# Second buffers for the operands of band attention, and half-size one-hot tiles for the expert gates, in a one-layer streaming encoder block

## The chip, the cores and the metric

One of the eight cores of a Trainium2 chip runs the whole program. The metric is the device time of one execution in microseconds (us); the result is told as the median of several runs. The five engines have queues of their own and run each queue strictly in order: PE (TensorE, matrix products), DVE (VectorE, elementwise work and reductions), ACT (ScalarE, activations and copies), POOL (GpSimd, which here only starts gathers) and SP (SyncE, which here starts every other transfer).

## The reference

The layer works on 1024 tokens of width 1024. Cut to what matters:

```python
h = modulate(rms_norm(x), shift1, scale1); proj = h @ w_in
o_a = chunked_band_attention(qa, ka, va)       # 8 heads of 64; a chunk of 64 sees itself and 8 before it
o_b = gated_delta_rule(conv(qkv_b), g, beta)   # 4 heads of 128, a state carried from chunk to chunk
x = x + gate1 * (concat(rms_norm(o_a), o_b) @ w_out)
h2 = modulate(rms_norm(x), shift2, scale2)
# experts: 8 heads pick 16 of 16384 single-neuron experts for each token
u, vv = expert_down[experts], expert_up[experts]
y = einsum("thk,thkd->td", gates * gelu(einsum("thkd,td->thk", u, h2)), vv)
out = x + gate2 * y
```

All matrices are float32.

## The kernel before

The 1024 tokens are eight tiles of 128. The program has two parts.

**The front** takes every tile through six stages, which the program calls lanes. P (`project`) makes the projections of one or two tiles and stores queries, keys and values to a scratch tensor `rec` in the chip's main memory. D (`delta`) is the gated delta rule of one tile, with the state from the tile before. M (`attention`) is the band attention of one tile. O (`output`) is the output projection, the second norm and the query projection. R (`choose`) picks the experts. Tiles 2 to 5 are dense: G (`gates_dense`) spreads their gates over all 16384 experts, into a scratch tensor `gd`. The other tiles gather the rows of their own experts, one row of 1024 numbers per token and slot: `down` (L901 gathers, L903 multiplies and sums) and then `up` (L915 gathers, L920 accumulates), 128 slots each. In the front stand `down` and `up` of tile 0 and `down` of tile 1.

**The dense part** runs all experts as matrix products for the four dense tiles (L982 and L1005) in 32 steps of four blocks of 128 experts, and beside them the gathers of tiles 1, 6 and 7. Its memory lies where the lanes' memory was.

The order of each queue is set when the program is built, by a scheduler: every lane has a priority (`PRI`, L56: M first, then D, O, P, R, G, and the gathers last), and the scheduler places the ready instruction of the best priority, as its own reckoning has it. On the chip nothing overtakes: an instruction that waits holds up all that stands behind it on its engine. A buffer of a lane is one slot of a named ring; its next tile may be written once the last reader of the tile before is done.

**Attention of one tile** (L510 to L569) runs four rounds, one for each pair of heads. A round loads queries, keys and values of its pair into `kv` (L517, L519; up to 11 blocks of 128 by 128) and the biases of the near band into `near` (L522), both rings of one slot. Then come the scores (L532), the bias and running maximum (L536), the exponential (L539), the transposes (L548, copied at L550), the product with the values (L556) and the scaled result (L559). The score products read `kv`, and L556 is its last reader. All of a tile's products go through one bank of PSUM (`BANKS`, M=1). L568 ends the tile. In the delta lane L663 ends the tile, and its ring `rg` had 12 slots (`RINGS`, 'D').

**The gates of a dense tile** (L851 to L885): for each block of 16 tokens, groups of `GQ` = 8 tokens are taken. Two one-hot tiles of 128 by 8x128 half-precision numbers are compared on DVE (L870); ACT scales one of them twice per token, by the upper and the lower part of the gate (L877); PE multiplies (L878, two products per token), and after every four tokens ACT copies the bank to `stg` (L881). After 16 tokens two transfers store `stg` (L885). A group takes four tiles of a ring of six (`RINGS`, 'G').

Of the kernel before, what the change touches and what calls it, by code (L numbers as in the profile page):

```python
# [20 lines left out]
F = mybir.dt.float32  # L21
BF = mybir.dt.float16
R = mybir.dt.float32r
# [7 lines left out]
P = 128  # L31
D = 1024
# [16 lines left out]
NROW = 3  # L49
NMORE = 4  # L50
NHELD = 2
RINGS = {'P': 4, 'D': 12, 'M': 4, 'O': 3, 'R': 2, 'G': 6}
XBUFS = {'P': 1, 'O': 2}
WBUFS = {'P': 4, 'O': 3}
STEP = 10000
# [7 lines left out]
SHIFT = {}  # L63
SLOPE = {}
BANKS = dict(P=2, D=2, M=1, O=2, R=1)
GQ = 8
GROUPS = [[0], [1, 2], [3, 4], [5, 6], [7]]
STARTS = [0, 16, 24] + [32 + 4 * k for k in range(5)] + [52 + k for k in range(8)]
LEVELS = (1, 2, 4, 8, 16, 32, 64)
# [49 lines left out]
def hybrid_layer(ctx, tc, a, out):  # L119
    nc = tc.nc  # L120
    V, A_, PE, G, SP = nc.vector, nc.scalar, nc.tensor, nc.gpsimd, nc.sync
# [34 lines left out]
    def lt(shape, dt, name, bufs, tag=None):  # L156
        return pools_[cur[0][0]].tile(list(shape), dt, name=name, tag=(tag or name) + cur[0], bufs=bufs)

    def rg(shape=(P, 512), dt=F):
        return lt(shape, dt, "rg", RINGS[cur[0]])  # L160

# [348 lines left out]
    def attention(t, mixT):  # L510
        m0 = max(0, 4 - t)
        nk = 5 - m0
        oa = rg()
        for p in range(4):
            cs = slice(p * P, (p + 1) * P)
            kv = lt([P, 11, P], F, "kv", 1)
            SP.dma_start(kv[:, 0, :], rec[QA, t][:, cs])  # L517
            for n, kind in ((1, KA), (6, VA)):
                SP.dma_start(kv[:, n + m0:n + 5, :],  # L519
                             rec[kind, t - 4 + m0:t + 1, :, cs].rearrange("m p c -> p m c"))  # L520
            near = lt([P, 2, 256], F, "near", 1)
            SP.dma_start(near, neard[:, 2 * p:2 * p + 2])  # L522
            ss_, rs = [], sm(2)
            for hh in range(2):
                hp = slice(hh * 64, hh * 64 + 64)
                s = lt([P, 640], F, "sx", 2)
                init = BIG
                for lo, hi, bias in ((m0, 3, farm[:, min(m0, 2) * P:]), (max(m0, 3), 5, near[:, hh, (max(m0, 3) - 3) * P:])):
                    if lo >= hi:
                        continue  # L530
                    ps = mm()
                    PE.matmul(ps[:, :(hi - lo) * P], kv[hp, 0, :],  # L532
                              kv[hp, 1 + lo:1 + hi, :].rearrange("p m c -> p (m c)"), start=True, stop=True,
                              skip_group_check=True)
                    mf = sm(1)
                    V.tensor_tensor_reduce(s[:, lo * P:hi * P], ps[:, :(hi - lo) * P], bias, -1.0, init, OP.add,  # L536
                                           OP.min, accum_out=mf)
                    init = mf
                A_.activation(s[:, m0 * P:], s[:, m0 * P:], AF.Exp, bias=mf, scale=-1.0, accum_out=rs[:, hh:hh + 1])  # L539
                ss_.append(s)  # L540
            yield
            blocks = [(hh, m) for hh in range(2) for m in range(m0, 5)]
            PT = {}
            for b0 in range(0, len(blocks), 4):
                part = blocks[b0:b0 + 4]
                pt = mm()
                for n, (hh, m) in enumerate(part):
                    PE.transpose(pt[:, n * P:(n + 1) * P], ss_[hh][:, m * P:(m + 1) * P], ident)  # L548
                d = rg()
                A_.activation(d[:, :len(part) * P], pt[:, :len(part) * P], AF.Copy)  # L550
                for n, bm in enumerate(part):
                    PT[bm] = d[:, n * P:(n + 1) * P]
            po = mm()
            for hh in range(2):
                for m in range(m0, 5):
                    PE.matmul(po[:, hh * 64:hh * 64 + 64], PT[hh, m], kv[:, 6 + m, hh * 64:hh * 64 + 64],  # L556
                              start=(m == m0), stop=(m == 4), skip_group_check=True)
            V.reciprocal(rs, rs)
            V.tensor_tensor(v3(oa[:, cs], 2), v3(po[:, 0:P], 2), b3(rs, AD), OP.mult)  # L559
            yield  # L560
        junk = rg()
        ss = sm(1)
        A_.activation(junk, oa, AF.Square, accum_out=ss)
        r = rsqrt(ss, 1, 1.0 / 512)
        A_.activation(oa, oa, AF.Copy, scale=r)
        ps = transpose4(oa)
        for j in range(4):
            A_.activation(mixT[:, j, :], ps[:, j * P:(j + 1) * P], AF.Copy, scale=mixg[:, j:j + 1])  # L568
        yield  # L569
# [281 lines left out]
    def gates_dense(t):  # L851
        e12, gt = GATE.pop(t)
        ps = mm()
        for n, src in enumerate((e12[:, 0], e12[:, 1], gt)):
            PE.transpose(ps[:, n * P:(n + 1) * P], src.rearrange("p h s -> p (h s)"), ident)

        keys = lt([P, 2, P], BF, "gkeys", 1)
        V.tensor_copy(keys, ps[:, 0:2 * P].rearrange("p (a b) -> p a b", a=2))
        parts = lt([P, 2, P], F, "gparts", 1)
        V.tensor_scalar(parts[:, 0, :], ps[:, 2 * P:3 * P], 16384.0, None, op0=OP.mult)  # L860
        ghalf = lt([P, P], BF, "ghalf", 1)
        V.tensor_copy(ghalf, parts[:, 0, :])
        V.tensor_tensor(parts[:, 1, :], parts[:, 0, :], ghalf, OP.subtract)
        for blk in range(8):
            stg = lt([P, P, 16], F, "stg", 1)
            for q in range(2):
                n0 = blk * 16 + q * GQ
                oh1, oh2, whi, wlo = (rg((P, GQ * P), BF).rearrange("p (n i) -> p n i", n=GQ) for _ in range(4))
                for oh, key in ((oh1, 0), (oh2, 1)):
                    V.tensor_tensor(oh, iota_n[:, None, :].to_broadcast([P, GQ, P]),  # L870
                                    keys[:, key, n0:n0 + GQ, None].to_broadcast([P, GQ, P]), OP.is_equal)
                for h in range(GQ // 4):
                    ps = mm()
                    for j in range(4):
                        n = 4 * h + j
                        for m, w in enumerate((whi, wlo)):
                            A_.activation(w[:, n, :], oh2[:, n, :], AF.Copy, scale=parts[:, m, n0 + n:n0 + n + 1])  # L877
                            PE.matmul(ps[:, j * P:(j + 1) * P], w[:, n, :], oh1[:, n, :], start=(m == 0),  # L878
                                      stop=(m == 1), skip_group_check=True)
                    c0 = GQ * q + 4 * h  # L880
                    A_.activation(stg[:, :, c0:c0 + 4], ps.rearrange("p (n i) -> p i n", i=P), AF.Copy,  # L881
                                  scale=2.0 ** -14)
                yield
            for hf in range(2):
                SP.dma_start(gd[DENSE.index(t) * 8 + blk, hf], stg[:, hf * 64:hf * 64 + 64, :])  # L885
# [209 lines left out]
```

## Time and profile before

| what | value |
|---|---|
| median of three runs | 3504.95 us |
| the three runs | 3506.4, 3490.28, 3504.95 us |
| the profiled execution | 3495.83 us, its span 3494.1 us |
| busy share of the span: PE, DVE, ACT, POOL | 86%, 78%, 38%, 37% |
| first product of the dense part | 1967.2 us after the span's start |
| TensorE clock granted, mean | 0.902 of full speed |

The span runs from the first to the last instruction. A busy time counts what an engine ran, not how well; a wait row names the engine and line that waited, and the one that came last of what it waited for. "Idle before" and waits of an engine matter only where that engine, or one that waits for it, sets the end. SPq is the queue of SP itself.

### The profile page before, as it was taken

The page shows a single profiled execution, that of the slowest core. Times are in us where ns is not written, and L with a number is a line of the kernel's source. Part 1 is how long each engine was busy: PE and PEld are TensorE (multiplying, and loading weights), DVE is VectorE, ACT ScalarE, POOL GpSimd, SP SyncE. Part 2 cuts the span into 40 slices and gives each one's busy share as a digit, 9 for nine tenths or more (in the row PEclk, how much of TensorE's full clock was granted, in tenths as well). Part 3 has the DMA queues.
Part 4 walks back from the last instruction along what each step waited for, and adds up shares of the span by engine and source line. Part 5 has one row for each costly group of instructions (what it writes and reads, how often), then busy time and mean ns, then how long its engine had stood idle before and what let it go on. Part 6 is the DMA issues. An engine that isn't in the chain of part 4 may idle for free.

```text
span 3494.1 us, 44943 instructions
## 1 busy us (share of the span) xinstructions
PE 3014.0 (86%) x15196; PEld 2482.1 (71%) x15196; DVE 2719.5 (78%) x6407; ACT 1316.2 (38%) x2833; POOL 1310.2 (37%) x1028
## 2 busy tenths in 40 slices
PE   7988868798887898576877699999999999999998
PEld 5677756677766787465756577877777777777777
DVE  3347668768899778993585888988888888889898
ACT  2333134233235663386767632222222222222222
POOL 0000333432333323430000155556655556655563
PEclk9988878899878899686878899999999999999999
DMA  8865888898777987773435699999999999999997
GB/s 283 284 215 174 274 282 267 270 336 280 261 250 230 354 297 261 258 250 125 157 119 176 218 345 334 344 341 339 328 330 336 344 337 349 335 333 355 344 332 283
DMA packets 375959, 989.71 MB, mean 283 GB/s; under 512 B 33440, under 2 KB 139296, under 8 KB 375728
## 3 DMA queue, kind: packets, MB, share of 16 engines
q0 software_dynamic: 147456, 536.94, 43.4%
q1 hardware_dynamic: 228272, 449.90, 37.6%
q8 instruction: 119, 1.95, 0.2%
q14 instruction: 112, 0.92, 0.1%
HBM read 924.84 MB, written 61.87 MB: 282 GB/s over the span
## 4 chain that ended last, share of the span: by engine, by line
PE 37%; DMA 26%; DVE 20%; issue 9%; ACT 5%; POOL 3%; SPq 0%; DVEq 0%; POOLq 0%; ACTq 0%
PE at L982 12%; DMA row<-in_peer_expert_down_dram,idx 8%; PE yk L1005 6%; PE mm L365 5%; PE yc L1005 4%; DVE row L903 4%; DMA row<-in_peer_expert_up_dram,idx 4%; DMA rawu<-in_peer_expert_up_dram 4%; DVE y L920 4%; PE mm L351 3%; DMA rawd<-_peer_expert_down_t_dram 2%; POOL row L901 2%; DMA g<-gd 2%; ACT rg L877 2%; DMA w<-in_w_ada_dram 1%
## 5 line engine op out<-in xcount | busy, mean ns | idle before, releaser
L901 POOL DMA_INDIRECT row<-in_peer_expert_down_dram,idx x512 | 645.5, 1261 | 1113.0 <-DVE s L310 353.7
L915 POOL DMA_INDIRECT row<-in_peer_expert_up_dram,idx x512 | 664.5, 1298 | 1035.5 <-DMA g<-gd 421.3
L903 DVE CUSTOM_DVE_ANT_0 row<-row,h2a 128x1024 f32<-128x1024 f32 x512 | 619.7, 1222 | 139.4 <-DMA row<-in_peer_expert_down_dram,idx 138.6
L920 DVE SCALAR_TENSOR_TENSOR y<-row,act,y 128x1024 f32<-128x1024 f32 x508 | 651.8, 1283 | 53.3 <-DMA row<-in_peer_expert_up_dram,idx 50.1
L877 ACT ACTIVATE rg<-rg,gparts 128x128 f16<-128x128 f16 x1024 | 318.3, 396 | 75.7 <-PE mm L878 49.0
L985 ACT ACTIVATE gl<-at 128x512 f32<-128x512 f32 x128 | 76.4, 597 | 670.8 <-PE at L982 670.8
L982 PE MATMUL at<-hhi,dhi 128*128 128x512 f32 x1024 | 260.6, 396 | 16.3 <-ACT dhi L963 16.2
L365 PE MATMUL mm<-h2T,w 128*128 128x256 f32 (+1 forms) x1280 | 251.8, 358 | 19.0 <-DMA w<-in_peer_w_query_dram 8.2
L982 PE MATMUL at<-hlo,dhi 128*128 128x512 f32 x1024 | 256.8, 392 | 0.0
L1005 PE MATMUL yk<-uhi,whi 128*128 128x512 f32 x512 | 202.5, 412 | 61.7 <-ACT whi L991 56.4
L351 PE MATMUL mm<-w,hT 128*128 128x256 f32 x1024 | 249.3, 398 | 7.3 <-DMA w<-in_w_in_dram 4.6
L982 PE MATMUL at<-hhi,dlo 128*128 128x512 f32 x1024 | 254.7, 389 | 0.7 <-DVE dlo L964 0.7
L365 PEld LDWEIGHTS mm<-h2T,w 128*128 128x128 f32 x1280 | 218.2, 205 | 44.7 <-DMA w<-in_peer_w_query_dram 9.7
L982 PEld LDWEIGHTS at<-hhi,dhi 128*128 128x128 f32 x1024 | 194.7, 191 | 60.1 <-ACT dhi L963 19.0
L351 PEld LDWEIGHTS mm<-w,hT 128*128 128x128 f32 x1024 | 199.2, 200 | 45.3 <-DMA w<-in_w_in_dram 6.4
L982 PEld LDWEIGHTS at<-hlo,dhi 128*128 128x128 f32 x1024 | 194.4, 190 | 41.0
L982 PEld LDWEIGHTS at<-hhi,dlo 128*128 128x128 f32 x1024 | 192.2, 188 | 41.0 <-DVE dlo L964 1.2
L1005 PE MATMUL yk<-ulo,whi 128*128 128x512 f32 x512 | 204.0, 404 | 3.5 <-DVE ulo L964 3.5
L1005 PE MATMUL yc<-uhi,whi 128*128 128x512 f32 x512 | 205.1, 401 | 0.5 <-DVE yacc L1014 0.5
L1005 PE MATMUL yc<-ulo,whi 128*128 128x512 f32 x512 | 204.2, 399 | 0.0
L1005 PE MATMUL yc<-uhi,wlo 128*128 128x512 f32 x512 | 199.5, 390 | 0.0
L870 DVE TENSOR_TENSOR rg<-iota_n,gkeys 128x1024 f16<-128x1024 f16 x128 | 151.0, 1222 | 55.9 <-PE mm L878 55.8
(300 smaller groups left out, 5582.1 us busy)
## 6 DMA issues: line engine op xcount, KB each, us to landing
w<-in_w_in_dram SPq DMA_DIRECT2D x140, 512.0 KB
rawd<-_peer_expert_down_t_dram SPq DMA_DIRECT2D x128, 512.0 KB
rawu<-in_peer_expert_up_dram SPq DMA_DIRECT2D x128, 512.0 KB
w<-in_peer_w_query_dram SPq DMA_DIRECT2D x80, 512.0 KB
gd<-stg SPq DMA_DIRECT2D x64, 512.0 KB
g<-gd SPq DMA_DIRECT2D x32, 1024.0 KB
w<-in_w_ada_dram SPq DMA_DIRECT2D x48, 512.0 KB
w<-in_w_out_dram SPq DMA_DIRECT2D x40, 512.0 KB
```

The source lines that it names most:

```text
L351: PE.matmul(ps[t][:, hf * 256:hf * 256 + 256], hT[:, k, tt * P:(tt + 1) * P], w[k], start=(k == 0), stop=(k == KD - 1), skip_group_check=True)
L365: PE.matmul(ps[:, (c % per) * W:(c % per + 1) * W], w[k][:, (c % 2) * P:(c % 2 + 1) * P], hT[:, k, :W], start=(k == 0), stop=(k == KD - 1) ...
L870: V.tensor_tensor(oh, iota_n[:, None, :].to_broadcast([P, GQ, P]), keys[:, key, n0:n0 + GQ, None].to_broadcast([P, GQ, P]), OP.is_equal)
L877: A_.activation(w[:, n, :], oh2[:, n, :], AF.Copy, scale=parts[:, m, n0 + n:n0 + n + 1])
L901: G.indirect_dma_start(out=r, out_offset=None, in_=a["peer_expert_down"], in_offset=bass.IndirectOffsetOnAxis(ap=idx[:, j:j + 1], axis=0))
L903: V.tensor_tensor_reduce(r, r, h2, 1.0, 0.0, OP.mult, OP.add, accum_out=act[:, j:j + 1])
L915: G.indirect_dma_start(out=row, out_offset=None, in_=a["peer_expert_up"], in_offset=bass.IndirectOffsetOnAxis(ap=idx[:, j:j + 1], axis=0))
L920: V.scalar_tensor_tensor(y, row, w[:, j:j + 1], y, op0=OP.mult, op1=OP.add)
L982: PE.matmul(ps, l[:, k, :], r[:, k, :], start=(n == 0), stop=(n == 3 * KD - 1))
L985: A_.activation(g, ps, AF.Gelu)
L1005: PE.matmul(ps, l[:, ts_], r[:, cs], start=(m == 0 and (s == 0 or not own)), stop=(m == 3 * SCN - 1 and (s == NK // SCN - 1 or not own)))
```

## The change

Three numbers and one loop bound change. `kv` and `near` get rings of two slots in place of one; this takes 7.5 KB of each partition's memory (5.5 and 2). The gate groups take `GQ` = 4 tokens in place of 8, so the six tiles of their ring have half the size (6 KB less), and a block of 16 tokens is four groups. The ring of the delta lane has 11 slots in place of 12 (2 KB less).

```diff
-RINGS = {'P': 4, 'D': 12, 'M': 4, 'O': 3, 'R': 2, 'G': 6}
+RINGS = {'P': 4, 'D': 11, 'M': 4, 'O': 3, 'R': 2, 'G': 6}
-GQ = 8
+GQ = 4
-            kv = lt([P, 11, P], F, "kv", 1)
+            kv = lt([P, 11, P], F, "kv", 2)
-            near = lt([P, 2, 256], F, "near", 1)
+            near = lt([P, 2, 256], F, "near", 2)
-            for q in range(2):
+            for q in range(16 // GQ):
                 n0 = blk * 16 + q * GQ
                 oh1, oh2, whi, wlo = (rg((P, GQ * P), BF).rearrange("p (n i) -> p n i", n=GQ) for _ in range(4))
```

The scheduler builds every queue anew, so instructions move on all engines. Two places show it.

On SP, the loads of the last attention round of the last tile (L517, L519), among the stores of gates (L885), the weights of the query projection (`w_query`) and of the output projection (`w_out`). Before:

```order
L198 DMA w<-in_w_out_dram 128x1024
L522 DMA near<-neard 128x512
L198 DMA w<-in_w_out_dram 128x1024 x2
L250 DMA rg<-gated 128x512
L885 DMA gd<-stg 128x1024 x2
L517 DMA kv<-rec 128x128
L519 DMA kv<-rec 128x5x128 x2
```

Now:

```order
L522 DMA near<-neard 128x512
L198 DMA w<-in_peer_w_query_dram 128x1024 x2
L885 DMA gd<-stg 128x1024 x2
L198 DMA w<-in_peer_w_query_dram 128x1024 x2
L517 DMA kv<-rec 128x128
L519 DMA kv<-rec 128x5x128 x2
L198 DMA w<-in_peer_w_query_dram 128x1024 x2
L885 DMA gd<-stg 128x1024 x2
L198 DMA w<-in_peer_w_query_dram 128x1024 x3
L198 DMA w<-in_w_out_dram 128x1024
```

The load has moved ahead of five loads of query weights and of the first output weights of tile 7, which stood in front of it.

On ACT, the seam between the last gates (L877, L881) and the first split weights of the dense part (`dhi`, L963), up to the first expert activation (L985). Before:

```order
L877 ACTIVATE rg<-rg,gparts 128x128 x6
L963 ACTIVATE dhi<-rawd 128x1024
L833 ACTIVATE gt<-gt 128x128
L881 ACTIVATE stg<-mm 128x128x4
L963 ACTIVATE dhi<-rawd 128x1024
L881 ACTIVATE stg<-mm 128x128x4
L963 ACTIVATE dhi<-rawd 128x1024
L985 ACT_TABLE_LOAD
```

Now:

```order
L963 ACTIVATE dhi<-rawd 128x1024
L877 ACTIVATE rg<-rg,gparts 128x128 x8
L833 ACTIVATE gt<-gt 128x128
L881 ACTIVATE stg<-mm 128x128x4
L877 ACTIVATE rg<-rg,gparts 128x128 x6
L881 ACTIVATE stg<-mm 128x128x4
L877 ACTIVATE rg<-rg,gparts 128x128 x2
L963 ACTIVATE dhi<-rawd 128x1024
L877 ACTIVATE rg<-rg,gparts 128x128 x4
L985 ACT_TABLE_LOAD
```

Before, no scaling (L877) and two copies (L881) stand behind the first `dhi`; now 56 scalings and eight copies do, most of them behind the rows shown here.

## Rows read from the trace of the kernel before

**Rows 1.** Stretches of the span: engine busy us (instructions), then granted clock, DMA share, GB/s.
```profile
0.00:340.00 340.00, 281.83 (x1844) 222.98 (x1844) 161.03 (x724) 104.72 (x238) 1.62 (x6) 0.93 0.71 239
340.00:1550.00 1210.00, 984.76 (x5326) 832.50 (x5327) 971.88 (x2915) 503.87 (x1215) 430.52 (x386) 0.85 0.81 276
1550.00:1967.00 417.00, 310.38 (x1877) 255.81 (x1875) 256.60 (x1040) 297.98 (x860) 8.85 (x3) 0.77 0.46 154
1967.00:3494.00 1527.00, 1437.04 (x6152) 1170.84 (x6152) 1330.03 (x1732) 409.63 (x522) 869.17 (x634) 0.98 0.93 334
```

**Rows 2.** Waits of DVE, 340 to 1550 us: total us, times, longest.
```profile
DVE row L903 <- DMA row<-in_peer_expert_down_dram,idx: 132.5, 93, 4.8
DVE y L920 <- DMA row<-in_peer_expert_up_dram,idx: 45.0, 37, 3.9
DVE sx L536 <- PE mm L532: 13.7, 13, 3.8
```

**Rows 3.** Chain that ended last, 1590 to 1615 us: start, us, what.
```profile
1593.25 4.54 PE mm L556 x20
1597.81 0.32 SPq L517
...
1598.19 3.32 DMA kv<-rec
...
1601.65 1.63 PE mm L532 x2
...
1608.96 0.48 ACT stg L881
...
1612.09 2.33 ACT rg L877 x8
```

**Rows 4.** PE in order of time, 1590 to 1830 us: start, us, then what it waited for.
```profile
1620.20 4.53 PE L556 MATMUL mm<-kv,rg 128*128 128x64 f32 x20 [1.01 <-ACT rg L550]
...
1646.57 0.91 PE L532 MATMUL mm<-kv 64*128 64x384 f32 x2
...
1789.35 4.53 PE L556 MATMUL mm<-kv,rg 128*128 128x64 f32 x20 [0.98 <-ACT rg L550]
...
1797.80 1.62 PE L532 MATMUL mm<-kv 64*128 64x384 f32 x2 [1.37 <-DMA kv<-rec]
```

**Rows 5.** Waits of SP's queue, whole span.
```profile
SPq L517 <- PE mm L556: 127.7, 26, 13.1
```

**Rows 6.** Groups by line and shape: count | busy us, mean ns | idle before.
```profile
L870 DVE TENSOR_TENSOR rg<-iota_n,gkeys 128x1024 f16<-128x1024 f16 x128 | 151.0, 1222 | 55.9 <-PE mm L878 55.8
...
L625 DVE TENSOR_TENSOR rg<-rg,level 128x512 f32<-128x512 f32 x48 | 32.9, 686 | 0.0
```

**Rows 7.** Stretches, L870 alone: us, DVE busy (instructions), clock, DMA.
```profile
340.00:1550.00 1210.00, 61.44 (x52) 0.85 0.81 276
1550.00:1967.00 417.00, 89.60 (x76) 0.77 0.46 154
```

**Rows 8.** PE in order of time, 1900 to 2010 us.
```profile
1967.20 3.55 PE L982 MATMUL at<-hhi,dhi 128*128 128x512 f32 x8 [1.69 <-ACT dhi L963]
...
1976.61 1.98 PE L982 MATMUL at<-hlo,dhi 128*128 128x512 f32 x8
```

**Rows 9.** Ends of delta (L663) and attention (L568): duration ns min/median/max, first and last start.
```profile
L663 ACT ACTIVATE mixT<-mm,mix_gain x8: 687/687/738, 180.2 to 1666.7; 128x512 f32<-128x512 f32 x8
...
L568 ACT ACTIVATE mixT<-mm,mix_gain x32: 347/361/386, 182.7 to 1837.6; 128x128 f32<-128x128 f32 x32
```

**Rows 10.** Waits of DVE, 1550 to 1967 us.
```profile
DVE rg L870 <- PE mm L878: 50.5, 20, 7.6
DVE rg L559 <- PE mm L556: 30.3, 3, 12.5
DVE sx L536 <- PE mm L532: 25.3, 12, 7.3
```

**Rows 11.** Waits of ACT, 1550 to 1967 us.
```profile
ACT rg L877 <- PE mm L878: 28.9, 17, 4.9
```

## The prediction, before the changed kernel was run

> **What bounds the kernel now.** I read the stretches first, because the span has four parts with different limits [rows 1]. Before 340 us the first tile is on its way and no gather runs yet. From 340 to 1550 us the 384 gathers of the front run. From 1550 to 1967 us the front ends without gathers. From 1967 us the dense part runs. [...]
>
> From 340 to 1550 us it is DVE. It is busy for 972 of 1210 us, which leaves 238 us idle, and 177.5 of those are waits for a gathered row, 132.5 for `down` and 45.0 for `up` [rows 2]. The reader should see what stands third: DVE waited only 13.7 us for the scores of attention. DVE runs in order, so attention can be late here by tens of us and DVE does other work meanwhile. [...] The dependences of the last tiles set the end: attention of tile 7 ends at 1837.6 us, its delta rule already at 1666.7 [rows 9], and output, choice and the last gates follow.
>
> **How attention is chained.** One round in the chain of waits [rows 3]: the product with the values runs from 1593.25 us for 4.54 us, SP starts the load at 1597.81, the third transfer lands 3.32 us after 1598.19, and the next scores start at 1601.65. From the end of one round's last product to the next round's first it is 3.9 us, and none of it is arithmetic. SP was itself held up by this: 26 times it stood at L517 until L556 was done, 127.7 us in all [rows 5], with every other load behind it.
>
> **The change part by part.** The sum is made against the profiled execution, 3495.8 us, which is 9.1 us below the median of the three runs.
>
> *Second slots, 1550 to 1967 us.* Five loads fall here, one for tile 6 and four for tile 7. From the end of L556 to the next L532 the gaps are 3.9 us at 1597.8, 21.8 us at 1624.7 (1620.20 plus 4.53 to 1646.57), and so on to 3.9 us at 1793.9; the first, the largest and the last are shown [rows 3, 4], and the five add to 43 us. In the 21.8 us PE had output work to do that was placed ahead, so not all of that gap is the load. The floor is five times 3.9, 19 us; the ceiling 43. I take 25, nearer the floor, since the other gaps are near it. SP's queue agrees in kind: the last load now stands ahead of six weight loads that stood in front of it. What is late next is the bank of PSUM, which L559 must empty before the next scores: it waited 30.3 us in this stretch, three times [rows 10], and that wait stays.
>
> *Second slots, 340 to 1550 us.* DVE sets the pace, so the gain is what DVE waited for attention: at most 13.7 us [rows 2]. The load is one part of what delayed those scores. Between 0 and 14 I take 10, since the load is the only part of a round that waits on no arithmetic. If the order of DVE's queue falls otherwise, the 177.5 us of gather waits can shift by some 20 us either way; that is in the range, not in the sum.
>
> *Second slots, before 340 us.* Tile 0 has three such loads, but this stretch is filled by weights (239 GB/s, PE busy 282 of 340 us [rows 1]). I take nothing, with up to 3 x 3.9 = 12 us as the other end; the weights hide it, and if they were there earlier the 12 us would come in.
>
> *Gate groups of four.* L870 goes from 128 instructions of 1024 elements, 1222 ns each, to 256 of 512. No row shows a half-precision compare of 512, so the bounds are half of 1222 (611) and the nearest row of that size, 686 ns for a float32 product of 512 [rows 6]. The pieces of 1024 cost the same as other elementwise work of that size, so I take 686: 2 x 686 - 1222 = 150 ns more for each old instruction. 52 of them lie in the DVE-bound stretch [rows 7]: 52 x 0.150 = 7.8 us on the path. 76 lie after it, 11.4 us, where DVE is 62% busy: 7 us. Together 15, between 0 and 19. ACT scales as often as before and copies as often, and PE multiplies as often; they cost nothing more.
>
> [...]
>
> *The seam.* 56 scalings and eight copies of the last gates now stand on ACT behind the first `dhi`, against two copies before. At 2.33 us for eight scalings and 0.48 us for a copy [rows 3] the extra is 16.3 + 6 x 0.48 = 19.2 us of ACT. The first four blocks give PE 12 x 1.98 = 24 us of L982 [rows 8] to do beside it, though PE needs ACT's `dhi` for each of them. The work is moved, not added. Cost between 0 and 19; I take 5. If PE runs out of L982, the load of the finished gates is what is late.
>
> *Delta ring of 11.* Delta of tile 7 ends 171 us before attention does [rows 9], and that cover pays for any wait for a slot. Nothing, and from the cover up to perhaps 10 us where its pieces hold up PE's queue.
>
> *Sum:* -25 - 10 + 15 + 5 = -15, so 3480.8 on the scale of the profiled execution, and 3489.9 on that of the median. I do not know on which of the two the new runs will lie, and predict the middle, **3485 us**, 0.57% below 3504.95. The measurement tells about 0.5%, 17.5 us, from no change.
>
> **The rivals.**
>
> *A. Attention's chain sets the whole front.* 26 of the 32 loads waited for the round before, and SP's 127.7 us of it [rows 5] are of the size of the loads. If it bounded the front, 28 loads after tile 0 at 3.9 us would come off: 109 us, 3387 on the profiled scale and 3391 in the middle between the scales. For it: delta, output and choice all wait on attention, and the end of tile 7's attention is what the end of the front hangs on. Against: DVE's waits for L536 are 13.7 us in 1210 [rows 2], so the 23 loads before 1590 us are covered. [...]
>
> *B. The hand-over of gate groups doubles; slower.* In the last stretch DVE stood 50.5 us, 20 times, at L870 until PE had freed a one-hot tile [rows 10], and ACT 28.9 us, 17 times, at L877 [rows 11]. If these waits come once per group, and not with the amount of work, twice the groups add up to 79 us. The ring still holds one and a half groups, but now in half the time. With DVE's 50.5 added and the rest of the sum as above it is 3480.8 + 50.5 = 3531, in the middle scale 3536; with both, 3565. It decides from the point where more than a third of these waits repeats with the group: a third of 79 is 26, more than the 15 gained. For it: the waits are long, 2.5 us on average, close to a group's scalings. Against: DVE waits there because PE is behind with other lanes' products, and a smaller piece is freed sooner.
>
> *C. The slots are there and nothing is won.* The bank of PSUM lets the next scores start only after L559, and where the new order puts other products first the gap stays as in the 21.8 us of tile 7 [rows 4]. Then the 25 and the 10 go, and the costs remain: from 3496 to 3516, about the old time.
>
> **How the numbers follow.** Forecast 0.50, A 0.12, B 0.20, C 0.18. With all ends and the 20 us of the gathers on one side, the forecast's own sum runs from -89 to +49; as they will not all fall alike, I give it 3455 to 3512. Half of it lies below 3487.5 (0.25), most of the rest within 0.5% (0.20), 0.05 above. A is faster in full (0.12); C is within in 0.11, slower in 0.04 and faster in 0.03; B is slower in 0.16 and within in 0.04. That gives faster 0.40, same 0.35, slower 0.25. The range reaches to B's middle and part of the way to A: 3430 to 3540, and leaves out most of A and the far half of B.
>
> **What would show it.** Right: the gaps from L556 to L532 are gone or hold only L559; SP hardly waits at L517; DVE waits for rows about as long as now until the gathers of `down` of tile 1 end, near 1540 us, and the first L982 comes about 15 us sooner, near 1952, with the dense part 1527 us long as before; L870 has 256 instructions near 0.69 us. Wrong: the stretch with gathers gets shorter by more than 30 us (A), or the waits of L870 and L877 grow with the number of groups (B). If the dense part itself gets longer or shorter by more than 10 us, a step is missing here altogether.

## The result, and the profile after

The changed kernel takes **3464.36 us** (median of six runs; the kernel before, run beside it, 3501.63). The ratio is 0.9889 with an interval of 0.9859 to 0.9919, so it is 1.1% faster. One of the six executions took 6936.44 us at a granted clock of 0.438; it counts in that median, which is 3462.05 us without it, and not in the ratio. The profiled execution took 3448.8 us, its span is 3446.2 us and the granted clock 0.907 (before: 3495.8, 3494.1, 0.902).

The stretches of after, cut at the same times except that the dense part now begins at 1916 us; they answer to [rows 1].

```profile
0.00:340.00 340.00, 276.97 (x1840) 219.91 (x1840) 156.74 (x715) 103.99 (x237) 3.99 (x8) 0.95 0.70 241
340.00:1550.00 1210.00, 1006.57 (x5392) 845.40 (x5392) 982.51 (x3006) 506.29 (x1199) 419.54 (x386) 0.85 0.82 281
1550.00:1916.00 366.00, 276.52 (x1764) 231.73 (x1764) 244.35 (x1071) 279.41 (x813) 0.94 (x1) 0.79 0.44 153
1916.00:3446.00 1530.00, 1439.82 (x6200) 1173.04 (x6200) 1339.85 (x1745) 430.03 (x584) 869.24 (x634) 0.97 0.92 335
```

The dense part is as long as before (1530 us against 1527). All of the gain lies ahead of it, and the reader should see in which form: between 340 and 1550 us PE does 1006.6 us of work where it did 984.8, and between 1550 us and the dense part it does 276.5 where it did 310.4. Work moved out of the last stretch into the one with the gathers, though not all of it: PE has 113 instructions fewer in the last stretch, 66 more in the one with the gathers and 48 more in the dense part. The ends of the lanes in the trace of after show the same (duration, then first and last start).

```profile
L901 POOL DMA_INDIRECT row<-in_peer_expert_down_dram,idx x128: 935/940/1954, 1104.3 to 1528.2; - x128
...
L663 ACT ACTIVATE mixT<-mm,mix_gain x8: 681/687/708, 178.3 to 1603.3; 128x512 f32<-128x512 f32 x8
...
L568 ACT ACTIVATE mixT<-mm,mix_gain x32: 347/364/378, 174.6 to 1782.5; 128x128 f32<-128x128 f32 x32
...
L365 PE MATMUL mm<-h2T,w x512: 274/379/794, 1629.8 to 1885.8; 128*128 128x256 f32 x86, 128*128 128x128 f32 x85
...
L982 PE MATMUL at<-hhi,dhi x1024: 387/389/796, 1916.4 to 3418.9; 128*128 128x512 f32 x171
```

The last gather of `down` of tile 1 starts at 1528.2 us, 11.5 us sooner than the 1539.7 of before, in the trace of before:

```profile
L901 POOL DMA_INDIRECT row<-in_peer_expert_down_dram,idx x128: 932/937/4822, 1109.0 to 1539.7; - x128
...
L365 PE MATMUL mm<-h2T,w x512: 275/379/582, 1695.7 to 1937.1; 128*128 128x256 f32 x86, 128*128 128x128 f32 x85
```

But delta of tile 7 ends 63 us sooner than in [rows 9] (1603.3 against 1666.7), its attention 55 us sooner (1782.5 against 1837.6), the query projection after 1550 us begins 66 us sooner (1629.8 against 1695.7), and the first dense product comes 50.8 us sooner than in [rows 8] (1916.4 against 1967.2). The gathers hardly ended sooner, and when they ended, the other lanes were further on. These numbers are of the whole change; what the second slot does in them by itself is told below, with the slot added to the groups.

**The loads.** In PE's order of time of after, the last round of tile 7 now follows the round before with no load between; this answers to [rows 4].

```profile
1720.79 1.23 PE L556 MATMUL mm<-kv,rg 128*128 128x64 f32 x10
...
1724.06 0.41 PE L556 MATMUL mm<-kv,rg 128*128 128x64 f32 x2
1725.79 0.91 PE L532 MATMUL mm<-kv 64*128 64x384 f32 x2
```

1724.06 plus 0.41 to 1725.79 is 1.3 us, against 3.9 before. The load for that round was issued at 1674.9 us, as the last start in SP's queue of after shows, as soon as the round two before it, the last reader of its slot, had done its products at 1674.9:

```profile
L517 SPq DMA_DIRECT2D kv<-rec x32: 319/326/532, 107.1 to 1674.9; - x32
```

Over the 21 rounds that follow another round of their tile in tiles 1 to 7, the gaps from the last L556 of a round to the first L532 of the next add up to 175 us before and 95 after (8.3 and 4.5 us each). SP still stands at L517, though; this answers to [rows 5]:

```profile
SPq L517 <- PE mm L556: 102.1, 21, 13.7
```

**VectorE's waits.** First from 340 to 1550 us, answering to [rows 2]: the scores of attention, 13.7 us before, are 1.5 us now, and the waits for gathered rows are as long as they were (138.7 and 44.9 us against 132.5 and 45.0).

```profile
DVE row L903 <- DMA row<-in_peer_expert_down_dram,idx: 138.7, 88, 4.9
DVE y L920 <- DMA row<-in_peer_expert_up_dram,idx: 44.9, 30, 4.7
DVE rg L870 <- PE mm L878: 9.9, 6, 3.9
DVE rg L559 <- PE mm L556: 5.4, 5, 1.6
```

Then from 1550 to 1916 us, answering to [rows 10]:

```profile
DVE rg L870 <- PE mm L878: 61.7, 26, 6.6
DVE sx L536 <- PE mm L532: 16.4, 6, 9.8
```

And ACT's in the same stretch, answering to [rows 11]:

```profile
ACT rg L877 <- PE mm L878: 51.1, 24, 5.4
ACT rg L877 <- DVE rg L870: 13.5, 17, 2.7
```

**The gate groups.** The one-hot compare, answering to [rows 6]:

```profile
L870 DVE TENSOR_TENSOR rg<-iota_n,gkeys 128x512 f16<-128x512 f16 x256 | 164.9, 684 | 76.1 <-PE mm L878 71.6 <-ACT rg L877 3.9 <-PE mm L351 0.5
```

684 ns for one of 512 elements, and 14 us more of VectorE's time in all (164.9 against 151.0).

### The profile page after: what moved, and what is told of

Read it like the earlier page. It is cut to its first block, busy times and chain, and to the rows that moved or that the text cites. A ratio compares the mean times of both kernels' runs of the same rounds, so it can differ in the third digit from the quotient of the medians.

```text
span 3446.2 us, 45156 instructions
## 1 busy us (share of the span) xinstructions
PE 2999.9 (87%) x15196; PEld 2470.1 (72%) x15196; DVE 2723.4 (79%) x6535; ACT 1319.7 (38%) x2830; POOL 1293.7 (38%) x1028
## 4 chain that ended last, share of the span: by engine, by line
PE 29%; DVE 10%; DMA 9%; issue 4%; ACT 3%; POOL 1%; DVEq 0%; ACTq 0%; POOLq 0%; SPq 0%
PE at L982 12%; PE yk L1005 6%; PE yc L1005 5%; DMA rawu<-in_peer_expert_up_dram 3%; PE mm L365 2%; DVE y L920 2%; DMA rawd<-_peer_expert_down_t_dram 2%; DMA g<-gd 2%; DVE row L903 1%; ACT rg L877 1%; PE mm L351 1%; DVE rg L870 1%; DVE ulo L964 1%; DMA row<-in_peer_expert_down_dram,idx 1%; DVE gl L988 1%
## 5 line engine op out<-in xcount | busy, mean ns | idle before, releaser
L901 POOL DMA_INDIRECT row<-in_peer_expert_down_dram,idx x512 | 633.9, 1238 | 1091.4 <-DVE act L903 335.7
L920 DVE SCALAR_TENSOR_TENSOR y<-row,act,y 128x1024 f32<-128x1024 f32 x508 | 650.8, 1281 | 48.8 <-DMA row<-in_peer_expert_up_dram,idx 44.9
L877 ACT ACTIVATE rg<-rg,gparts 128x128 f16<-128x128 f16 x1024 | 330.3, 395 | 117.3 <-PE mm L878 64.7
L985 ACT ACTIVATE gl<-at 128x512 f32<-128x512 f32 x128 | 76.4, 597 | 672.8 <-PE at L982 665.3
L982 PE MATMUL at<-hhi,dhi 128*128 128x512 f32 x1024 | 257.3, 393 | 15.7 <-ACT dhi L963 15.7
L870 DVE TENSOR_TENSOR rg<-iota_n,gkeys 128x512 f16<-128x512 f16 x256 | 164.9, 684 | 76.1 <-PE mm L878 71.6
```

Of the source, the lines that this page charges most:

```text
L901: G.indirect_dma_start(out=r, out_offset=None, in_=a["peer_expert_down"], in_offset=bass.IndirectOffsetOnAxis(ap=idx[:, j:j + 1], axis=0))
L920: V.scalar_tensor_tensor(y, row, w[:, j:j + 1], y, op0=OP.mult, op1=OP.add)
L982: PE.matmul(ps, l[:, k, :], r[:, k, :], start=(n == 0), stop=(n == 3 * KD - 1))
L985: A_.activation(g, ps, AF.Gelu)
```

## The experiments

Each kernel is the one before with the edit shown. "Groups of four" means this part of the change, which the later diffs don't repeat:

```diff
-GQ = 8
+GQ = 4
-            for q in range(2):
+            for q in range(16 // GQ):
```

The second slot was run only with groups of four, which free the memory that it takes; what it does beside groups of eight is not shown. Each ratio is to the kernel before, run beside the kernel in question.

### Groups of four alone (e1), with the ring of 11 (e2), and the ring of 11 alone (e3)

```diff
-RINGS = {'P': 4, 'D': 12, 'M': 4, 'O': 3, 'R': 2, 'G': 6}
+RINGS = {'P': 4, 'D': 11, 'M': 4, 'O': 3, 'R': 2, 'G': 6}
```

The first has groups of four without this line, the second has both, the third this line alone.

> Gate groups of four alone; the kernel before in all else (one slot for keys and values and for near biases, delta ring of 12). Theory S (the second slots bring the whole gain): this is 0 to 0.5% slower than the kernel before, 3502 to 3519 us, from 15 us more of L870. Theory G (the smaller groups bring it, because shorter pieces stand in the queues of DVE and ACT): 0.7 to 1.2% faster, 3460 to 3477 us. Theory O (any edit makes the scheduler build another order, and the parts do not add up): anywhere within 1% on either side, with another split over the stretches than the change has.

> Gate groups of four and the delta ring of 11, one slot each for keys and values and for near biases: the change without its second slots. Theory S: 0 to 0.5% slower than the kernel before (3502 to 3519 us), so that the second slots are worth 1.1 to 1.6% against it. Theory G: as fast as the change, 3455 to 3475 us. Theory O: within 1% on either side, not near the run with groups alone.

> The delta ring of 11 alone. Theory S: no difference, within 0.3% (3491 to 3512 us), since delta ends 171 us before attention in the last tile. A theory D, that the smaller ring brings the gain by spacing delta out (delta of tile 7 took 224 us before and 190 in the change): 0.5 to 1% faster. Theory O: a difference of up to 1% in either direction.

Measured: 3490.41 us, ratio 0.9982 (0.9963 to 1.0001); 3486.73 us, 0.9973 (0.9953 to 0.9992); 3504.12 us, 1.0003 (0.9983 to 1.0023). None of the three differs from the kernel before by more than 0.3%. The groups cost nothing that can be seen, and the ring of the delta lane neither costs nor brings anything. The waits around the groups did grow: with the groups alone VectorE and ACT waited like this from 1550 to 1955 us, against 50.5 us in 20 waits [rows 10] and 28.9 us in 17 [rows 11].

```profile
DVE rg L870 <- PE mm L878: 68.6, 35, 6.6
...
ACT rg L877 <- PE mm L878: 48.6, 21, 5.4
ACT rg L877 <- DVE rg L870: 27.5, 14, 10.4
```

So VectorE's waits nearly doubled in number, ACT's grew too, and no time was lost: these waits did not set the end.

### A second slot for keys and values, with groups of four (e4)

```diff
-            kv = lt([P, 11, P], F, "kv", 1)
+            kv = lt([P, 11, P], F, "kv", 2)
```

> Two slots for keys and values, one for near biases, gate groups of four, delta ring of 12. Theory S: 0.7 to 1.1% faster than the kernel before (3463 to 3477 us), nearly all of the change's gain, as the near biases were already loaded before the round's first scores end. If the near slot matters as much as the other: 0.2 to 0.6% faster. Theory G: like the run with groups alone. Theory O: unrelated to either.

Measured: 3454.17 us, ratio 0.9874 (0.9851 to 0.9898). This one number is the whole of the change: the interval lies clear of that of the groups alone and overlaps that of the full change, so the second slot of `near`, with the ring of 11, brings nothing that can be seen. Against the groups alone the ratio falls by 0.0108, some 38 us. Where they come from, in the traces, first with the groups alone, then with the slot added:

```profile
L901 POOL DMA_INDIRECT row<-in_peer_expert_down_dram,idx x128: 932/938/1948, 1104.4 to 1522.8; - x128
...
L568 ACT ACTIVATE mixT<-mm,mix_gain x32: 349/367/394, 182.8 to 1823.5; 128x128 f32<-128x128 f32 x32
...
L982 PE MATMUL at<-hhi,dhi x1024: 387/389/796, 1955.4 to 3461.8; 128*128 128x512 f32 x171
```

```profile
L901 POOL DMA_INDIRECT row<-in_peer_expert_down_dram,idx x128: 936/938/1955, 1107.0 to 1529.9; - x128
...
L568 ACT ACTIVATE mixT<-mm,mix_gain x32: 346/365/379, 173.0 to 1783.9; 128x128 f32<-128x128 f32 x32
...
L982 PE MATMUL at<-hhi,dhi x1024: 387/389/796, 1920.8 to 3426.3; 128*128 128x512 f32 x171
```

The gathers end 7 us later with the slot, the first dense product comes 34.6 us sooner. What stands between them, the end of the front without gathers, shrank from 433 to 391 us. From 340 to 1550 us PE does 21.5 us more work with the slot; the groups alone first:

```profile
340.00:1550.00 1210.00, 990.74 (x5334) 835.62 (x5332) 979.60 (x2984) 498.10 (x1192) 422.24 (x390) 0.85 0.82 279
```

```profile
340.00:1550.00 1210.00, 1012.20 (x5392) 848.51 (x5392) 981.20 (x3001) 505.05 (x1194) 413.90 (x384) 0.84 0.82 279
```

Attention of tile 5, which ends well before the last gather, is done 45 us sooner with the slot (1368.0 against 1413.5), and the last product with the values of tile 7 comes 47 us sooner (1757.0 against 1804.2): nearly all of the lead is there while the gathers still run. Delta of tile 7 ends 41 us sooner and its query projection begins 43 us sooner. The gaps between rounds fell from 161 to 92 us, so 69 us of gaps gave 35 us of time.

### The loads made longer, in one slot (e5) and in two (e6)

Keys and values are loaded twice in each round, into the same place, so that a round's load takes longer while the work stays; the order of the queues is built anew. One kernel adds this to the groups alone, the other to the groups with the second slot.

```diff
-            for n, kind in ((1, KA), (6, VA)):
+            for n, kind in ((1, KA), (6, VA), (1, KA), (6, VA)):
```

> Gate groups of four, one slot for keys and values, delta ring of 12 (the run e1_groups_only), and every round loads its keys and values twice into the same place, the second time after the first. Theory L (what the second slot hides is the load's latency in attention's chain): about 3.5 us more in each of the 28 rounds after tile 0, 98 us in the chain; from e1 to e4 the gaps inside the tiles shrank by 69 us and the time by 36, so about half comes through: 3525 to 3550 us. Theory Q (what counts is that SP no longer stands at L517 with weight loads behind it): SP stands there for the product either way, and the doubled load costs only its two starts, under 1 us a round: 3490 to 3505 us.

> The same doubling in the kernel with two slots for keys and values (the run e4_kv_slot_and_groups). Theory L: the second load is hidden too, 3450 to 3470 us, so that the distance between e5 and this grows to some 70 us. A theory T (the doubled bytes and starts cost by their traffic, wherever they lie): as much over e4 as e5 is over e1.

Measured: 3531.62 us, ratio 1.0077 (1.0048 to 1.0105), in one slot; 3440.27 us, 0.9831 (0.9791 to 0.9871), in two. In one slot the load's length is on the path: the gaps grow from 161 to 291 us and the ratio by 0.0095, 33 us. That is within theory L's range and outside theory Q's. In two slots the same extra transfers cost nothing at all (the interval overlaps that without them). That speaks against theory T; the time lies 10 us under what theory L gave. So what the change bought is the time of the load: make the load longer, and only the kernel with one slot pays. The first dense product with doubled loads, in one slot and then in two:

```profile
L982 PE MATMUL at<-hhi,dhi x1024: 387/389/796, 1986.7 to 3504.3; 128*128 128x512 f32 x171
```

```profile
L982 PE MATMUL at<-hhi,dhi x1024: 387/389/794, 1888.5 to 3402.8; 128*128 128x512 f32 x171
```

Without the doubling it was 1955.4 and 1920.8. In one slot it comes 31 us later; in two it even comes 32 us sooner, of which the dense part takes 24 back (3445.1 - 1888.5 = 1557 us against 1533). The doubled loads also gave the scheduler a new order of the queues, and 32 us is nearly as much as the slot's own 35, so the order remains a rival for the size of the gain (theory O). Its sign stands on three comparisons: the slot added to single loads (38 us faster) and to doubled loads (0.0246 of the base, 86 us faster), and the load doubled in one slot (33 us slower). SP's waits at L517 for the two kernels with doubled loads, one slot first:

```profile
SPq L517 <- PE mm L556: 122.5, 27, 12.3
```

```profile
SPq L517 <- PE mm L556: 158.8, 24, 13.2
```

The faster kernel waits longer there. How long SP stands at this line does not tell whether the load is on the path.

How much of a gap comes through is not one share. The sums of gaps above leave out the first round of each tile, whose gap holds other work; with these and with tile 0 they lead to the last product with the values of tile 7. Adding the slot took 69 us from the gaps, 9 us from the rounds themselves (1006 to 997 us in the 28 rounds of tiles 1 to 7) and 6 us from tile 0, but added 37 us ahead of first rounds: that product ended 47 us sooner, and the first dense product came 35 us sooner. Doubling the load in one slot added 130 us of gaps and 18 us in tile 0, and took 67 us from the rounds (to 939) and 47 us ahead of first rounds: 34 us later, and the first dense product 31. In both, close to one half of the gaps and rounds arrived (35 of 78 us, 31 of 63), but out of different terms, so the half is no rule.

Where the slot lost its part can be seen ahead of tile 3. Tile 2 was done 14 us sooner, but the projection had the keys of the next two tiles stored (L499) 24 us later, and the first scores of tile 3 (L532) came 25 us later. SP and PE in order of time, with the groups alone and then with the slot:

```profile
703.76 1.93 SPq L499 DMA_DIRECT2D rec<-rg  x2
715.73 0.70 PE L532 MATMUL mm<-kv 64*128 64x256 f32 x2 [0.57 <-DMA kv<-rec]
```

```profile
727.39 0.65 SPq L499 DMA_DIRECT2D rec<-rg  x1
729.23 1.60 SPq L499 DMA_DIRECT2D rec<-rg  x1
740.58 0.70 PE L532 MATMUL mm<-kv 64*128 64x256 f32 x2
```

This one gap went from 43.5 to 82.1 us.

### A fourth row buffer for the gathers (e7), and then one less in the dense part (e9)

The gathers of the front use three row buffers in turn (`NROW`); the dense part adds four (`NMORE`). Both kernels have groups of four and one slot.

```diff
-NROW = 3
+NROW = 4
```

```diff
-NROW = 3
-NMORE = 4
+NROW = 4
+NMORE = 3
```

> The memory that groups of four free given to a fourth row buffer for the gathers instead; one slot for keys and values. The prediction read DVE's waits for gathered rows, 177 us between 340 and 1550 us, as what sets that stretch's pace besides DVE's work. If so, a fourth buffer takes off a good part of them: 40 to 100 us, 3390 to 3450 us, and the gathers of the front end well before 1500 us. If the pace there comes from the front's other work and the gathers only fill, the waits go but the time stays: 3475 to 3495 us.

> The run e7 (groups of four, one slot for keys and values, a fourth row buffer) with three instead of four further row buffers in the dense part, so that seven serve the gathers there as before. In e7 the front ended 68 us sooner than in e1 but the dense part took 1591 us against 1533, with 76 us of waits of L1005 for whi. Theory B (the eighth buffer lets gathers run ahead and their traffic and DVE work hold up the weights): the dense part is back near 1535 us with the front as in e7, 3420 to 3435 us. Theory M (a front that ends sooner only moves what the dense part must wait for, gates and experts of the last tiles): 3465 to 3485 us as in e7.

Measured: 3472.16 us, ratio 0.99 (0.9868 to 0.9932), with the fourth buffer, and 3416.87 us, 0.9768 (0.9734 to 0.9802), when the dense part also keeps the seven it had. VectorE's waits for rows in the kernel with four and four, 340 to 1550 us:

```profile
DVE row L903 <- DMA row<-in_peer_expert_down_dram,idx: 77.3, 62, 4.5
DVE y L920 <- DMA row<-in_peer_expert_up_dram,idx: 39.9, 28, 4.9
```

117 us, against 181 with three buffers and the groups alone (127.3 and 53.3). The last gather of `down` of tile 1 starts at 1401.7 us in place of 1522.8 and the first dense product comes at 1887.2 in place of 1955.4, 68 us sooner. So VectorE's waits for rows were on the path of this stretch: 64 us of them went, and the front became as much shorter. Nothing shows that VectorE's own work held it: with the groups alone it was busy there for 980 us in place of 972, and yet the last gather of `down` of tile 1 started 17 us sooner than in the kernel before (1522.8 against 1539.7). That attention could not shorten the stretch fits this; no run shows it by itself. The time with the fourth buffer lies between its two expected ranges, because the dense part grew; the time with seven in the dense part lies 3 us under theory B's.

The first of the two kernels gives most of the 68 us back: its dense part takes 3478.2 - 1887.2 = 1591 us, against 1533 with the groups alone. With seven buffers there it is 3416.6 - 1887.3 = 1529. PE's waits from 1890 us on, with eight and with seven:

```profile
PE yk L1005 <- ACT whi L991: 76.0, 28, 11.6
PE at L982 <- ACT dhi L963: 40.0, 15, 5.3
```

```profile
PE yk L1005 <- ACT whi L991: 55.5, 18, 11.5
PE at L982 <- ACT dhi L963: 14.1, 9, 2.3
```

46 of the 62 us stand in these two rows. That the eighth buffer does it is shown; through what (the order of the queue, or the gathers running further ahead of the weights) is not.

### Both together (e8, e10, e11)

Each of three kernels has the second slot and the fourth row buffer, and pays for them with other buffers. All have groups of four, `NROW = 4`, the second slot of keys and values, a ring of 11 for the delta lane and one slot in place of two for the tile `wk` of the choice lane. The first also shortens the gate ring and keeps eight buffers in the dense part; the other two keep seven there, leave the gate ring at six, raise the gate lane's number in `PRI` from 5000 to 6000, and shorten the ring of the output lane or that of the projection lane:

```diff
-RINGS = {'P': 4, 'D': 12, 'M': 4, 'O': 3, 'R': 2, 'G': 6}
+RINGS = {'P': 4, 'D': 11, 'M': 4, 'O': 3, 'R': 2, 'G': 5}
```

```diff
-RINGS = {'P': 4, 'D': 12, 'M': 4, 'O': 3, 'R': 2, 'G': 6}
+RINGS = {'P': 4, 'D': 11, 'M': 4, 'O': 2, 'R': 2, 'G': 6}
-WBUFS = {'P': 4, 'O': 3}
+WBUFS = {'P': 4, 'O': 2}
```

```diff
-RINGS = {'P': 4, 'D': 12, 'M': 4, 'O': 3, 'R': 2, 'G': 6}
+RINGS = {'P': 3, 'D': 11, 'M': 4, 'O': 3, 'R': 2, 'G': 6}
```

> Both: two slots for keys and values and a fourth row buffer, paid with a delta ring of 11, a gate ring of five and one work tile of the top-16 search in place of two. If the two gains lie in different waits they add: 36 us under e7. If attention's chain is hidden once DVE runs ahead, or the gate ring of five costs more than it gives: no better than e4, 3450 to 3470 us.

> Two slots for keys and values and four row buffers (three more in the dense part), paid with a delta ring of 11, one work tile of the top-16 search, and an output ring of two; the gate ring has its six tiles. e8 ended its front at 1855 us, 66 us before e4, but 103 us of gates stood behind it with a ring of five. Theory B and a gate ring that mattered: front near 1860 us and a dense part near 1540, 3400 to 3420 us. If the smaller output ring holds up tiles 5 to 7: a front near 1920, 3450 us or more.

> As e10, but a projection ring of three instead of the output ring of two. The projection of tiles 5 and 6 released attention of tile 5 in the change, so a smaller projection ring should hold the front up more than the output ring does if it binds: 10 to 40 us slower than e10. If neither binds, as fast as e10, 3400 to 3420 us.

Measured: 3509.44 us, ratio 1.0037 (1.0011 to 1.0063); 3448.68 us, 0.9851 (0.9814 to 0.9889); and **3396.2 us, 0.9708 (0.9674 to 0.9742)**. The last beats the kernel before by 2.9% and the change by 1.8% of the same base. I had expected a projection ring of three to be the dearer of the two payments; it is the cheaper one.

The first of the three is slower than the kernel before and lies above both times expected for it, and the second lies between its two ranges. These kernels differ in several numbers at once, so no single one of them is shown as a cause.

One thing shows beside their times: where the first dense product stands against the last compare of the gates (L870). In the kernel with the gate ring of five they lie at 1854.9 and

```profile
L870 DVE TENSOR_TENSOR rg<-iota_n,gkeys x256: 639/686/694, 1135.1 to 1957.7; 128x512 f16<-128x512 f16 x128
```

103 us apart, with the gates behind. In its first 150 us the dense part has PE at work for 98.6 us, and it is 1660 us long; but this kernel also has the eighth row buffer, which cost 62 us above. In the fastest kernel the pair is 1811.4 and 1882.4,

```profile
L870 DVE TENSOR_TENSOR rg<-iota_n,gkeys x256: 666/689/744, 1117.3 to 1882.4; 128x512 f16<-128x512 f16 x128
...
L982 PE MATMUL at<-hhi,dhi x1024: 387/389/795, 1811.4 to 3370.1; 128*128 128x512 f32 x171
```

71 us apart, and its dense part takes 3397.1 - 1811.4 = 1586 us. With the output ring of two it is 71 us and 1590, and in the kernel with four and three buffers of the section before, which has seven there as well, 25 us and 1529. The front of the fastest kernel became 156 us shorter and the kernel 97 us (3494.1 against 3397.1). So these kernels agree with the reading that a front that ends ahead of its gates hands the rest on to the dense part; the raised number in `PRI`, which puts the gates later, is part of that, and was not tried alone.

### Groups of four with a ring of twelve (e12)

```diff
-RINGS = {'P': 4, 'D': 12, 'M': 4, 'O': 3, 'R': 2, 'G': 6}
+RINGS = {'P': 4, 'D': 12, 'M': 4, 'O': 3, 'R': 2, 'G': 12}
```

> Groups of four tokens as in the run with the groups alone, but with twelve one-hot tiles in the ring in place of six: the ring then covers 48 tokens again, as in the kernel before, while VectorE still issues 256 instructions for them. It asks which of the two sides of the smaller groups is there at all: the prediction charged +15 us for the 128 more instructions and +5 us for the shorter lead of the ring; the groups alone measured a ratio of 0.998 (0.9963 to 1.0001). Theory R (VectorE's waits at L870 for TensorE's L878, 73.3 us in 40 waits with six tiles against 55.8 us in 24 before, are waits for a free tile, and the shorter ring costs something that the smaller pieces give back elsewhere): with twelve tiles the waits at L870 fall below 30 us, the first dense product comes 10 to 20 us before the 1955.4 us of the groups alone, and the ratio is 0.993 to 0.996. Theory T (TensorE's own place in its queue sets when those products run; VectorE waits because it has nothing else to do): the waits stay between 45 and 80 us, the first dense product lies within 8 us of 1955, and the ratio is 0.997 to 1.000, the same as with six tiles. If the 128 more instructions were worth their 15 us and the shorter ring had been a gain, this run would be slower than the kernel before by 0.3% or more.

Measured: 3467.73 us, ratio 0.9901 (0.9863 to 0.9939). VectorE's waits at L870 over the whole span, with twelve tiles:

```profile
DVE rg L870 <- PE mm L878: 69.6, 39, 7.2
```

With six it was 73.3 us in 40 waits. Twice the tiles left the wait as it was, and the first dense product at 1954.9 us (1955.4), as theory T says: the length of the ring is not what VectorE waits for there. The ratio fits neither: it lies 0.7 points under T's range, and where its interval reaches into R's, R's two other signs are missing. The profiled execution has the difference in the dense part, 3468.2 - 1954.9 = 1513 us against 1533, where PE waits less for `dhi`:

```profile
PE yk L1005 <- ACT whi L991: 39.1, 23, 4.1
...
PE at L982 <- ACT dhi L963: 7.9, 5, 2.1
```

against 51.3 and 29.9 us with the ring of six. Why a longer gate ring changes the dense part is open.

## Why the prediction was right, and where it was not

The direction and the forecast's own range held: 3464 us lies within 3430 to 3540 and within the 3455 to 3512 of the likeliest case. The gain was twice the one predicted, 1.1% against 0.57%.

**The sum.** It was -25 - 10 + 15 + 5. The two gains, 35 us together, are the size of what was measured: 35 us of the first dense product and some 38 us of the median between the groups alone and the groups with the slot. That is luck in part, since neither was made in the way that the sum says. The two charges, 20 us together, did not show: the groups alone measured -0.2%, between -0.4% and nothing. Without them the sum is -35; the medians differ by 37 us, the profiled executions by 47.

**Second slots, 1550 to 1967 us.** The 25 us came to 42 between the last gather and the first dense product (433 to 391, the slot added to the groups), close to the ceiling of 43, but not for the reason given. The step said that the gaps of tiles 6 and 7 would close. Of the five, the four other than the largest are 3.9, 4.1, 9.7 and 3.9 us before and 10.9, 1.6, 8.8 and 1.3 after, 21.6 against 22.6 in sum: nothing was won in them. The 21.8 us gap at the start of tile 7 [rows 4], which the step suspected of being PE's order and not the load, is 21.5 now: that suspicion was right.

**Second slots, 340 to 1550 us.** This is the step that failed: "the gain is what DVE waited for attention: at most 13.7 us". For the length of this stretch it holds, since the gathers ended within 12 us of where they did. But a stretch whose length is fixed can still hold more work. While the gaps of tiles 1 to 6 closed, PE did 22 us more of its work in there (in the change and from the slot alone), and the ends of attention and of the lanes that hang on it came some 55 to 65 us sooner in the change, 40 to 47 from the slot alone. Attention of tile 5 had 45 of these before the gathers ended. The gain was made in this stretch and collected in the next, where no gather covers the front.

**Gate groups of four.** The price of a compare was right (686 taken, 684 measured), and with it that 512 elements cost more than half of 1024. The choice of the row had luck in it: the trace of before also has a half-precision product of that size, at 424 ns, under the lower bound of 611 that the prediction took.

```profile
L820 DVE TENSOR_TENSOR rg<-rg 128x512 f16<-128x512 f16 x32 | 12.9, 424 | 0.0
```

The step that failed put 7.8 us of the compares "on the path" because VectorE was busy for 972 of 1210 us. With the groups alone VectorE was busy 8 us longer there and the gathers ended no later, and the fourth row buffer showed that waits for rows were on the path; that the extra compares fell into such waits is the likely reading. The single instruction did become dearer for its size: 684 ns at 512 elements is 56% of the 1222 ns at 1024.

**The seam.** 5 us were charged; over the whole span PE's wait for `dhi` was 16.2 us before and 15.7 after, and the dense part took 1530 us. The cover named, the first dense products, was enough.

**The ring of 11** was put at nothing and measured at nothing, with the groups and alone.

**The signs.** L870, the length of the dense part and the row waits came as said. "SP hardly waits at L517" was wrong: 102.1 us remain, because a load now waits for the round two before its own; inside the tiles it is issued 48 us ahead of the end of the round before its own, on average, so this wait holds up no round of attention. The first dense product was put near 1952 and came at 1916.

**The rivals.** A, attention's chain as the bound of the whole front, asked for 109 us and for a stretch of gathers shorter by over 30: it was shorter by 12. As a bound A falls. As a mechanism it was underrated: 69 us less of gaps gave 35 us, a doubled load costs 33 us in one slot and nothing in two, and the argument against it, that VectorE's waits cover the loads, was the failed step above. B has its sign and not its price: the waits at L870 and L877 went from 50.5 and 28.9 us to 61.7 and 51.1, with the groups alone to 68.6 and 48.6, and no time was lost. C falls with the gaps that closed and with the doubled loads.

**What stays open:** why the eighth row buffer lengthens the dense part, why a gate ring of twelve shortens it, why the projection of tiles 3 and 4 stores its keys later with the slot, and how much of the 35 us another order of the queues would give or take.

## What to carry to other kernels

Where one stage holds the length of a stretch (here the gathers), ask of a change to another stage not only whether it shortens the stretch, but how much further the other work is when the stretch ends; what gets done earlier under a fixed cover is collected where the cover ends (here attention of tile 5 was done 45 us sooner under the gathers, and the first dense product came 34.6 us sooner). Whether a transfer is on the path can be tried by making it longer: loading the same data twice told in two runs (33 us slower in one slot, no slower in two) what no length of a wait row had. And charge an engine's extra work to the path only after seeing that its own work, and not what it waits for, sets the pace (with the groups alone VectorE was 8 us busier, and the last gather of `down` of tile 1 started 17 us sooner).

## What the runs showed that I had not expected

- A queue's waits say nothing of cost by themselves: SP stood at L517 for 122.5 us in the slowest kernel of the doubled loads and for 158.8 us in the one that was 2.5 points faster.
- One buffer more for gathered rows, three to four, took 68 us from the front and 64 us from the waits for rows; one more in the dense part, seven to eight, cost that part 62 us.
- TensorE's granted clock stayed where it was through all of this in the stretch with gathers (0.85 before, after, and with the groups alone); in pieces of 20 us of that stretch of after it reads from 0.50 to 1.00. The fastest kernel, with PE busy for 1039 of those 1210 us in place of 985, has 0.88 there.
